# Second feed-forward product and second norm of a decoder layer: partial sums in a tile of their own, operand splits placed by another rule, norm bias copied in DRAM and added to by transfers, part of the statistics on ScalarE

## The chip, the cores and the metric

The kernel runs on one core of one Trainium2 chip. The metric is the device time of one execution in microseconds (us); the median of the runs shown is compared. The work is in float32: each matrix operand is held as a high and a low part (`both`, `wh`/`wl`, in fp32r), and each product is three matmuls (`mm3`, lines 113 to 115: high by high, high by low, low by high).

## The reference, cut to what matters

The layer normalises twice. The change is in the last two lines, `h @ w_ff2` and the second `layer_norm`.

```python
D_MODEL = 2048; SEQ = 512; D_FF = 4 * D_MODEL; ALPHA = 2 ** 0.25; LN_EPS = 1e-5

def layer_norm(x, gain, bias):
    mu = jnp.mean(x, axis=-1, keepdims=True)
    var = jnp.mean(jnp.square(x - mu), axis=-1, keepdims=True)
    return (x - mu) * lax.rsqrt(var + LN_EPS) * gain + bias

proj = x @ w_in[l]
...                      # gated recurrence, windowed attention, merged by gates
x = layer_norm(ALPHA * x + mixed @ w_out[l], ln1_gain[l], ln1_bias[l])
h = jnp.square(jax.nn.relu(x @ w_ff1[l])) @ w_ff2[l]
x = layer_norm(ALPHA * x + h, ln2_gain[l], ln2_bias[l])
```

## The kernel before

The stages run one after the other: projection of x, recurrence and attention, gates, `w_out` with the first norm, first feed-forward product, second feed-forward product, second norm. The instruction streams of the engines are laid out by a scheduler from the source; each engine then works through its stream in order, and SyncE (SP), ScalarE (ACT) and GpSimd (POOL) also issue transfers in their order.

**Start.** SyncE loads the first weight (`raw`, four pieces of 128 KB, line 97) and the first quarter of x (`xr`, four pieces of 256 KB, line 98), then x by 512 KB (line 185) and the weights by 512 KB (line 91). ScalarE writes the high part of each (`wh`, `both`, line 83), VectorE the low part (`wl`, line 84).

**Second feed-forward product** (from about 1950 us). The 512 tokens by 8192 rows of `h` lie in DRAM as `hd0` to `hd31`. There are 16 superblocks `s` of two `hd` each. For the output columns 0 to 1023 a superblock takes seven products instead of eight (`seven(s, i)`, i = 0 to 6; `product` makes 12 matmuls, of 128x512) on sums and differences of the operands. The columns 1024 to 2047 are done in the plain way, by `plain_unit` of 12 matmuls, one beside each `seven`. The operands of a superblock are made by `form(s, step)`: step -1 loads two `hd` into `raws[s]`, which is a pair tile for the first superblock and `HR0`, `HR1` (part of `slot`) for all others; steps 0 and 1 split them, 2 and 3 make sums, 4 and 5 split these. `A_RING` (four entries) and `S_RING` (two) hold the splits.

The results of the seven products are evacuated (`both_banks`: ACTIVATE at line 1052 or an addition at line 605) into four tiles `E`, `U2`, `T2`, `RX` of 128x1024, and `add_z` (line 956) adds them to `zq`, which holds the residual in DRAM, by accumulating transfers on GpSimd's queue. `E` serves two of them in each superblock: at i = 1 for `zq[0][0]` and at i = 4, as the partial sum U3, for `zq[1][1]`. ScalarE evacuates the plain columns' banks at line 1026.

**LAST** is the last plain block, columns 1536 to 2047 by the last three superblocks: 4 token tiles of 36 matmuls, straight in front of the second norm, with six weight tiles (`kept`).

**Second norm.** For each token tile `t` and column quarter `q`, `zq` is loaded to `zt[t, q]` on ScalarE's queue (line 1133). VectorE makes `bn_stats` of three quarters (line 1147), adds the bank `O[t]` of LAST to the fourth and makes its statistic (line 1149). `ln_core` gives the mean and 1/deviation (lines 830 to 838). Then mean, gain and bias are applied by all three of ScalarE (1156, 1160), VectorE (1157, 1159, 1164) and GpSimd (1159, 1161), and the quarters go out (line 1165). Gain and bias rows are loaded, broadcast, to E, U2, T2, RX (line 1136).

In the first feed-forward product the class `Sevens` uses tiles from `tmp` for partial sums, of 128x256.

## Time and profile before

| | us |
|---|---|
| median of 3 runs | 2648.18 |
| their range | 2646.94 to 2650.42 |
| the profiled execution | 2650.56 |
| its span in the trace | 2648.70 |
| TensorE busy in it | 2594.6 (98%) |
| VectorE, ScalarE, GpSimd busy | 1872.9, 1285.5, 261.4 |
| first matmul, last matmul's start | 5.00, 2625.86 |

The span is from the first to the last instruction of the profiled execution; its own time is 1.86 us longer. A row of a timeline gives the start, the duration, the engine, the source line, the operation with the tiles that it writes and reads, and in brackets how long the engine was idle before it and who released it. Queue rows (SPq, ACTq, POOLq) are transfers being issued. The busy time is an average over stages with different limits, so the places where TensorE is idle are looked up one by one.

### The profile page before, as it was taken

To read this page: it belongs to the slowest core of one execution; us is meant where nothing else is said; L and a number is where in the kernel's file an instruction comes from. 1 tells how busy PE (TensorE), PEld (TensorE's weight loads), DVE (VectorE), ACT (ScalarE), POOL (GpSimd) and SP (SyncE) were. 2 spreads that over 40 slices of the span, in tenths; PEclk is the share of its full clock that TensorE was granted. 3 is DMA by queue.
4 is the path that set the end of the run, shared out by engine and by line. 5 is a ranking of instruction groups with operands and counts; after the bars stand their busy time and mean duration, and the time that the engine had idled before them with its cause. 6 is when DMAs were issued, how large, how long until landed. Compare 5 with 4: busy or idle time off the path is not lost.

```text
span 2648.7 us, 36998 instructions
## 1 busy us (share of the span) xinstructions
PE 2594.6 (98%) x14624; PEld 2260.5 (85%) x14624; DVE 1872.9 (71%) x2531; ACT 1285.5 (49%) x1815; POOL 261.4 (10%) x276
## 2 busy tenths in 40 slices
PE   9999999999999999999999999999999999999995
PEld 8889888988888999988988999999988888877884
DVE  4588795574635888833768888888886777766756
ACT  4576655352433444422545455455565555544542
POOL 0110222130000000000300000000001111101112
PEclk9999999999999999999999999999999999999998
DMA  5222212222454555643552333333368887878866
GB/s 190 88 80 72 78 57 88 73 80 81 158 183 151 158 161 155 243 137 98 174 189 104 135 135 129 136 136 127 136 209 214 215 205 206 223 183 206 208 160 173
DMA packets 110318, 392.84 MB, mean 148 GB/s; under 512 B 12480, under 2 KB 13248, under 8 KB 109376
## 3 DMA queue, kind: packets, MB, share of 16 engines
q1 hardware_dynamic: 79200, 281.40, 31.6%
q0 software_dynamic: 24896, 91.24, 15.2%
q10 hardware_dynamic: 6048, 17.83, 2.1%
q8 instruction: 115, 1.88, 0.3%
q14 instruction: 59, 0.48, 0.1%
HBM read 299.19 MB, written 91.23 MB: 147 GB/s over the span
## 4 chain that ended last, share of the span: by engine, by line
PE 86%; DVE 5%; issue 4%; DMA 3%; ACT 1%; POOL 1%; SPq 0%; DVEq 0%; ACTq 0%; POOLq 0%
PE mm L115 17%; PE mm L113 16%; PE mm L114 16%; PE mm L662 8%; PE tp L662 5%; PE mm L664 4%; PE tp L114 4%; PE tp L113 4%; PE tp L115 4%; PE tp L664 2%; DMA zq<-slot 1%; PE sc L114 1%; PE sc L115 1%; PE sc L113 1%; DMA slot<-hd 1%
## 5 line engine op out<-in xcount | busy, mean ns | idle before, releaser
L83 ACT ACTIVATE wh<-raws 128x1024 fp32r<-128x1024 f32 x292 | 307.9, 1059 | 331.6 <-PE mm L114 107.5
L84 DVE TENSOR_TENSOR wl<-raw,wh 128x1024 fp32r<-128x1024 f32 (+1 forms) x183 | 221.4, 1210 | 306.0 <-PE mm L115 167.1
L84 DVE TENSOR_TENSOR wl<-raws,wh 128x1024 fp32r<-128x1024 f32 x292 | 354.3, 1220 | 61.4 <-ACT wh L83 51.7
L83 ACT ACTIVATE wh<-raw 128x1024 fp32r<-128x1024 f32 (+1 forms) x183 | 190.9, 1044 | 294.1 <-PE mm L114 142.7
L115 PE MATMUL mm<-both,wl 128*128 128x512 f32 (+1 forms) x912 | 331.0, 364 | 2.1 <-DVE wl L84 2.1
L113 PE MATMUL mm<-both,wh 128*128 128x512 f32 (+1 forms) x912 | 331.0, 364 | 2.0 <-ACT wh L83 1.2
L114 PE MATMUL mm<-both,wh 128*128 128x512 f32 (+1 forms) x912 | 331.3, 364 | 0.0
L662 PE MATMUL mm<-both,wh 128*128 128x512 f32 x896 | 321.8, 398 | 0.4 <-ACT wh L83 0.4
L664 PE MATMUL mm<-both,wl 128*128 128x256 f32 x896 | 251.3, 281 | 0.0
L113 PE MATMUL mm<-wh,both 128*128 128x256 f32 (+1 forms) x688 | 231.9, 340 | 5.7 <-ACT both L83 5.0
L114 PE MATMUL mm<-wl,both 128*128 128x256 f32 (+1 forms) x688 | 232.3, 338 | 4.2 <-DVE wl L84 4.2
L115 PE MATMUL mm<-wh,both 128*128 128x256 f32 (+1 forms) x688 | 231.0, 338 | 0.0
L662 PEld LDWEIGHTS mm<-both,wh 128*128 128x128 f32 x896 | 168.6, 188 | 37.6 <-ACT wh L83 0.6
L115 PEld LDWEIGHTS mm<-both,wl 128*128 128x128 f32 x912 | 172.0, 189 | 28.2 <-DVE wl L84 2.8
L113 PEld LDWEIGHTS mm<-both,wh 128*128 128x128 f32 x912 | 172.1, 189 | 28.0 <-ACT wh L83 1.4
L114 PEld LDWEIGHTS mm<-both,wh 128*128 128x128 f32 x912 | 172.2, 189 | 25.4 <-DVE both L84 0.2
L113 PE MATMUL mm<-xq,wh 128*128 128x256 f32 x672 | 190.4, 283 | 1.4 <-ACT wh L83 0.9
L115 PE MATMUL mm<-xq,wl 128*128 128x256 f32 x672 | 190.2, 283 | 0.1
L114 PE MATMUL mm<-xq,wh 128*128 128x256 f32 x672 | 190.1, 283 | 0.0
L664 PEld LDWEIGHTS mm<-both,wl 128*128 128x128 f32 x896 | 169.4, 189 | 0.5
L113 PEld LDWEIGHTS mm<-wh,both 128*128 128x128 f32 x688 | 131.4, 192 | 19.9 <-ACT both L83 5.0
L114 PEld LDWEIGHTS mm<-wl,both 128*128 128x128 f32 x688 | 131.6, 192 | 17.9 <-DVE wl L84 4.7
(313 smaller groups left out, 6082.0 us busy)
## 6 DMA issues: line engine op xcount, KB each, us to landing
raws<-w SPq DMA_DIRECT2D x178, 512.0 KB, 4.5
raw<-win SPq DMA_DIRECT2D x87, 512.0 KB, 3.6
zq<-slot POOLq DMA_DIRECT2D x63, 512.0 KB, 7.8
slot<-w SPq DMA_DIRECT2D x62, 512.0 KB, 6.1
raws<-wg SPq DMA_DIRECT2D x56, 512.0 KB, 4.4
raw<-wo SPq DMA_DIRECT2D x32, 512.0 KB, 3.6
hd<-r POOLq DMA_DIRECT2D x32, 512.0 KB, 2.9
zq<-r POOLq DMA_DIRECT2D x31, 512.0 KB, 8.3
```

Of the source, the lines that this page charges most:

```text
L83: ACT.activation(hi, src, AF.Copy)
L84: DVE.tensor_tensor(lo, src, hi.bitcast(F32), op=ALU.subtract)
L113: PE.matmul(o, ah, bh_, start=first, stop=False, skip_group_check=True)
L114: PE.matmul(o, ah, bl_, start=False, stop=False, skip_group_check=True)
L115: PE.matmul(o, al, bh_, start=False, stop=last, skip_group_check=True)
L662: PE.matmul(o[:].rearrange("p (i t) -> p i t", i=2), wh[:, k, :], x.two(k), start=first and k == 0, stop=False, skip_group_check=True)
L664: PE.matmul(o[:, :CG], wl[:, k, :], x.hi[:, k, :], start=False, stop=last and k == 7, skip_group_check=True)
```

## The change

1. `Sevens` takes its partial sums from one tile `sums` of five parts, instead of from five buffers of a pool.
2. In the second feed-forward product the partial sum U3 goes to the first four parts of `sums`, no longer to `E`.
3. `form` is called by another rule: the second superblock's operands go to a pair of their own, and from the fourth superblock on the steps are written one unit later. In the last superblock the products 5 and 6 change places.
4. Ahead of the product three DRAM tiles `od` are filled with the bias row of the second norm, one row for each of the 128 tokens. Of the first three token tiles, (x - mean) * gain / deviation is added to `od` by accumulating transfers, and `od` is then copied to the output. The fourth tile gets gain and bias on VectorE.
5. The statistics of two quarters of four per tile are made on ScalarE: a sum (ACTIVATE Copy), its negative, and a sum of squares around it (`triple`).
6. The loads of `zq` go to SyncE's queue.

```diff
-    def tmp(tag, bufs):
-        return pf.tile([P, CG], F32, tag=tag, bufs=bufs, name=nm(tag))[:]
+    sums = pf.tile([P, 5, CG], F32, name="sums")
+
+    def tmp(i, n):
+        return sums[:, i + n, :]
...
+    U3 = sums[:, :4, :].rearrange("p n t -> p (n t)")
...
         if step == -1:
-            if s < 1:
+            if s < 2:
...
-            both_banks(E, EA, False)
-            both_banks(E, EB, True)
-            add_z(1, 1, E)
+            both_banks(U3, EA, False)
+            both_banks(U3, EB, True)
+            add_z(1, 1, U3)
...
+    od = [pd.tile([P, D], F32, name=f"od{t}") for t in range(NT - 1)]
+    for o_ in od:
+        nc.scalar.dma_start(out=o_[:], in_=lnv[3, :].partition_broadcast(P))
+    st2 = pl.tile([P, NT, 6, 3], F32, name="st2")
+    for q in range(2):
+        DVE.memset(st2[:, :, q, 0:1], float(T))
...
-        v = u + 2
-        if v // 7 + 1 < NS and v % 7 < 6:
-            form(v // 7 + 1, v % 7)
-        if v % 7 == 6 and v // 7 + 2 < NS:
-            form(v // 7 + 2, -1)
-        seven(s, i)
+
+        if u < 4:
+            form(1, u + 2)
+        if 2 <= u < 8:
+            form(2, u - 2)
+        if s > 1 and i and s + 1 < NS:
+            form(s + 1, i - 1)
+        if i == 6 and 2 < s + 2 < NS:
+            form(s + 2, -1)
+        seven(s, i if s < NS - 1 else (0, 1, 2, 3, 4, 6, 5)[i])
...
-            nc.scalar.dma_start(out=zt[t, q], in_=zq[q][t // 2][:, t % 2, :])
-    for r in range(2):
-        for i in range(2):
-            nc.gpsimd.dma_start(out=gb2[2 * r + i], in_=lnv[2 + r, i * 1024:(i + 1) * 1024].partition_broadcast(P))
...
+            nc.sync.dma_start(out=zt[t, q], in_=zq[q][t // 2][:, t % 2, :])
+    for i in range(2):
+        nc.gpsimd.dma_start(out=(E, U2)[i], in_=lnv[2, i * 1024:(i + 1) * 1024].partition_broadcast(P))
+        nc.gpsimd.dma_start(out=(T2, RX)[i], in_=lnv[3, i * 1024:(i + 1) * 1024].partition_broadcast(P))
...
+    def triple(t, q):
+
+        junk, nmean = S_RING[(NS - 1) % 2][2][:, :T], pl.tile([P, 1], F32, tag="nmean", bufs=2, name=nm("nmean"))
+        ACT.activation(junk, zt[t, q], AF.Copy, scale=1.0 / T, accum_out=st2[:, t, q, 1:2])
+        ACT.activation(nmean[:], st2[:, t, q, 1:2], AF.Copy, scale=-1.0)
+        ACT.activation(junk, zt[t, q], AF.Square, bias=nmean[:], accum_out=st2[:, t, q, 2:3])
...
-        for q in range(3):
-            DVE.bn_stats(stats[:, t, q, :], zt[t, q])
-        tt(zt[t, 3], O[t][:], zt[t, 3], ALU.add)
-        DVE.bn_stats(stats[:, t, 3, :], zt[t, 3])
...
+        for q in range(2):
+            triple(t, q)
+        for q in range(2, 4):
+            if q == 3:
+                tt(zt[t, q], O[t][:], zt[t, q], ALU.add)
+            DVE.bn_stats(st2[:, t, 2 * q - 2:2 * q, :].rearrange("p a b -> p (a b)"), zt[t, q])
...
+        for q in range(4):
+            zc = zt[t, q]
+            DVE.scalar_tensor_tensor(zc, zc, mu, block_of((E, U2)[q // 2], q), op0=ALU.subtract, op1=ALU.mult)
+            if t < NT - 1:
+                ACT.activation(zc, zc, AF.Copy, scale=y)
+                nc.gpsimd.dma_start(out=od[t][:, q * T:(q + 1) * T], in_=zc, accum_op=ALU.add)
+            else:
+                DVE.scalar_tensor_tensor(zc, zc, y, block_of((T2, RX)[q // 2], q), op0=ALU.mult, op1=ALU.add)
+                (nc.sync if q % 2 else nc.scalar).dma_start(out=out[t * P:(t + 1) * P, q * T:(q + 1) * T], in_=zc)
+        if t < NT - 1:
+            nc.sync.dma_start(out=out[t * P:(t + 1) * P, :], in_=od[t][:])
```

What it moves is seen in the built order of each engine. A row has its place, the source line, the operation and its tiles.

**The start, ScalarE and SyncE.** ScalarE's first rows, before:

```order
1 L192 ACT_TABLE_LOAD
2 L192 ACTIVATE warm<-warm 128x1
3 L83 ACTIVATE wh_97<-raw_96 128x256
4 L83 ACTIVATE both<-xr_95 128x512
5 L83 ACTIVATE wh_97<-raw_96 128x256
```

and now (`lnv` holds the norms' rows, `od` the copies):

```order
1 L1095 DMA od_17607<-lnv 128x2048
2 L192 ACT_TABLE_LOAD
3 L192 ACTIVATE warm<-warm 128x1
4 L1095 DMA od_17608<-lnv 128x2048
5 L83 ACTIVATE wh_97<-raw_96 128x256
6 L1095 DMA od_17609<-lnv 128x2048
7 L83 ACTIVATE both<-xr_95 128x512
8 L83 ACTIVATE wh_97<-raw_96 128x256
```

The three copies stand between ScalarE's first instructions. SyncE's first loads with the semaphores that they wait for (DMAHW0 to 7 tell that a transfer has landed, and go round), before:

```order
5 L97 DMA raw_96<-win 128x256
6 L98 DMA xr_95<-xt 128x512
7 L97 DMA raw_96<-win 128x256
8 L98 DMA xr_95<-xt 128x512
9 L185 DMA xr_171<-xt 128x1024 [waits DMAHW0_49]
10 L185 DMA xr_171<-xt 128x1024 [waits DMAHW1_49]
11 L91 DMA raw_182<-win 128x1024 [waits DMAHW2_49]
```

and now:

```order
5 L97 DMA raw_96<-win 128x256
6 L98 DMA xr_95<-xt 128x512 [waits DMAHW0_49]
7 L97 DMA raw_96<-win 128x256 [waits DMAHW1_49]
8 L98 DMA xr_95<-xt 128x512 [waits DMAHW2_49]
9 L185 DMA xr_171<-xt 128x1024 [waits DMAHW3_49]
10 L185 DMA xr_171<-xt 128x1024 [waits DMAHW4_49]
11 L91 DMA raw_182<-win 128x1024 [waits DMAHW5_49]
```

The loads are the same, but three of the eight semaphores of the first round belong to the copies (0, 3 and 5), so that waiting begins three rows earlier.

**The middle, ScalarE**, where row 1447 is the evacuation at 2420.14 us of the trace before (`slot_17720` holds E, U2, T2 and RX, `slot_17721` the raw operands and weights):

```order
1446 L83 ACTIVATE wh_20939<-raws_20619 128x1024
1447 L1052 ACTIVATE slot_17720<-tp_17722 128x512
1448 L83 ACTIVATE both<-slot_17721 128x1024
1449 L1052 ACTIVATE slot_17720<-tp_17723 128x512
1450 L83 ACTIVATE wh_20958<-slot_17721 128x1024
1451 L1026 ACTIVATE slot_17720<-mm_17726 128x512
1452 L1026 ACTIVATE slot_17720<-mm_17727 128x512
1453 L83 ACTIVATE both<-slot_17721 128x1024
1454 L1052 ACTIVATE r_17731<-tp_17722 128x512
1455 L1052 ACTIVATE r_17731<-tp_17723 128x512
```

and now:

```order
1447 L83 ACTIVATE wh_20820<-raws_20498 128x1024
1448 L1055 ACTIVATE sums<-tp_17597 128x512
1449 L83 ACTIVATE both<-slot_17596 128x1024
1450 L1055 ACTIVATE sums<-tp_17598 128x512
1451 L83 ACTIVATE wh_20839<-slot_17596 128x1024
1452 L1029 ACTIVATE slot_17595<-mm_17601 128x512
1453 L1029 ACTIVATE slot_17595<-mm_17602 128x512
1454 L83 ACTIVATE both<-slot_17596 128x1024
1455 L1055 ACTIVATE r_17606<-tp_17597 128x512
1456 L1055 ACTIVATE r_17606<-tp_17598 128x512
```

The rows stand in the same order; two evacuations go to `sums` instead of `slot`.

**The end, VectorE**, the splits of LAST's weights (`wl`) and the first statistics, before:

```order
2322 L84 TENSOR_TENSOR wl_21978<-slot_17721,wh_21977 128x1024
2323 L1147 BN_STATS stats<-raws_22006 128x6
2324 L84 TENSOR_TENSOR wl_21983<-slot_17721,wh_21982 128x1024
2325 L605 TENSOR_TENSOR slot_17720<-tp_17724,slot_17720 128x512
2326 L605 TENSOR_TENSOR slot_17720<-sc_17725,slot_17720 128x512
2327 L84 TENSOR_TENSOR wl_21988<-slot_17721,wh_21987 128x1024
2328 L1147 BN_STATS stats<-raws_21996 128x6
2329 L84 TENSOR_TENSOR wl_21993<-slot_17721,wh_21992 128x1024
2330 L1147 BN_STATS stats<-raws_22001 128x6
2331 L1147 BN_STATS stats<-raws_22006 128x6
2332 L1147 BN_STATS stats<-raws_22011 128x6 x2
```

and now:

```order
2323 L605 TENSOR_TENSOR sums<-tp_17599,sums 128x512
2324 L605 TENSOR_TENSOR sums<-sc_17600,sums 128x512
2325 L84 TENSOR_TENSOR wl_21863<-slot_17596,wh_21862 128x1024
2326 L84 TENSOR_TENSOR wl_21868<-slot_17596,wh_21867 128x1024
2327 L605 TENSOR_TENSOR slot_17595<-tp_17599,slot_17595 128x512
2328 L605 TENSOR_TENSOR slot_17595<-sc_17600,slot_17595 128x512
2329 L84 TENSOR_TENSOR wl_21873<-slot_17596,wh_21872 128x1024
2330 L1177 BN_STATS st_17613<-raws_21881 128x6
2331 L84 TENSOR_TENSOR wl_21878<-slot_17596,wh_21877 128x1024
2332 L1177 BN_STATS st_17613<-raws_21886 128x6
2333 L1177 BN_STATS st_17613<-raws_21891 128x6
2334 L605 TENSOR_TENSOR raws_21881<-mm_17601,raws_21881 128x512
```

Of these rows two statistics stood ahead of a split (2323, 2328); now one does (2330), on the first token tile's third quarter, loaded from `zq`.

## Rows read from the trace of the kernel before

**Rows 1.** The page's first part, TensorE: busy us (share of the span) xinstructions

```profile
PE 2594.6 (98%) x14624; PEld 2260.5 (85%) x14624; DVE 1872.9 (71%) x2531; ACT 1285.5 (49%) x1815; POOL 261.4 (10%) x276
```

**Rows 2.** Timeline at the start: start us, us, engine, line, operation [idle before <-releaser]

```profile
5.00 0.58 PE L113 MATMUL mm<-wh,both 128*128 128x256 f32 x1 [5.00 <-ACT both L83]
...
13.18 1.06 ACT L83 ACTIVATE wh<-raw 128x1024 fp32r<-128x1024 f32 x1
```

**Rows 3.** Windows at the start: us, busy of each engine, PEclk, DMA share, GB/s

```profile
14.00:16.00 2.00, 0.95 (x5) 0.75 (x6) 1.73 (x2) 1.66 (x4) 0.00 (x0) 1.00 1.03 420
...
24.00:26.00 2.00, 2.00 (x19) 2.00 (x18) 0.01 (x1) 0.00 (x0) 0.00 (x0) 1.00 0.99 383
```

**Rows 4.** Timelines of TensorE, then ScalarE, in the second feed-forward product

```profile
2354.78 0.73 PE L113 MATMUL tp<-wh,both 128*128 128x512 f32 x2 [1.88 <-ACT wh L83]
...
2446.95 0.73 PE L113 MATMUL tp<-wh,both 128*128 128x512 f32 x2 [2.53 <-ACT wh L83]
...
2420.14 0.60 ACT L1052 ACTIVATE slot<-tp 128x512 f32<-128x512 f32 x1 [2.49 <-DMA zq<-slot]
...
2443.92 1.06 ACT L83 ACTIVATE both<-slot 128x1024 fp32r<-128x1024 f32 x1 [9.82 <-DMA slot<-hd]
```

**Rows 5.** Windows in the same product and at its end

```profile
2100.00:2110.00 10.00, 9.03 (x38) 6.63 (x37) 8.16 (x10) 3.41 (x5) 0.86 (x1) 1.00 0.68 188
2350.00:2360.00 10.00, 8.12 (x29) 6.20 (x28) 6.47 (x7) 5.68 (x7) 1.12 (x2) 0.83 0.51 108
...
2590.00:2600.00 10.00, 6.56 (x22) 4.87 (x21) 4.15 (x5) 3.77 (x5) 3.14 (x4) 0.83 1.03 222
```

**Rows 6.** Timeline of TensorE in LAST, from its first matmul to its last

```profile
2586.74 0.39 PE L113 MATMUL mm<-both 128*128 128x512 f32 x1
...
2594.79 0.80 PE L114 MATMUL mm<-wl,both 128*128 128x512 f32 x1 [3.44 <-DVE wl L84]
...
2601.92 0.50 PE L114 MATMUL mm<-wl,slot 128*128 128x512 f32 x1 [0.95 <-DVE wl L84]
...
2623.36 0.39 PE L113 MATMUL mm<-wh,slot 128*128 128x512 f32 x1
...
2625.86 0.39 PE L115 MATMUL mm<-wh,slot 128*128 128x512 f32 x1
```

**Rows 7.** Timelines of VectorE, then ScalarE, beside LAST

```profile
2592.92 0.69 DVE L1147 BATCH_NORM_STATS2 stats<-raws 128x6 f32<-128x512 f32 x1 [10.64 <-DMA raws<-zq]
2593.53 1.21 DVE L84 TENSOR_TENSOR wl<-slot,wh 128x1024 fp32r<-128x1024 f32 x1
...
2590.69 1.09 ACT L1026 ACTIVATE r<-mm 128x512 f32<-128x512 f32 x2
```

**Rows 8.** Timelines of VectorE, then ScalarE, behind the last matmul

```profile
2636.68 0.69 DVE L1149 BATCH_NORM_STATS2 stats<-raws 128x6 f32<-128x512 f32 x1
2637.41 0.26 DVE L830 BATCH_NORM_AGGREGATE mv<-stats 128x2 f32<-128x24 f32 x1
2637.71 0.15 DVE L831 TENSOR_SCALAR mv<-mv 128x1 f32<-128x1 f32 x1
...
2643.25 1.40 DVE L1164 SCALAR_TENSOR_TENSOR raws<-raws,mv,slot 128x512 f32<-128x512 f32 x2
...
2640.42 0.72 ACT L1160 ACTIVATE raws<-raws,mv 128x512 f32<-128x512 f32 x1 [0.42 <-DVE mv L837]
```

**Rows 9.** DMA issues: out<-in, queue, operation xcount, KB each, median us to landing

```profile
zq<-slot POOLq DMA_DIRECT2D x63, 512.0 KB, 7.8
...
z<-xn ACTq DMA_DIRECT2D x4, 1024.0 KB, 8.2
zq<-z POOLq DMA_DIRECT2D x16, 256.0 KB, 4.6
raws<-zq ACTq DMA_DIRECT2D x16, 256.0 KB, 7.7
...
out<-raws SPq DMA_DIRECT2D x8, 256.0 KB, 2.4
```

More of the change, by code (lines that the diff above doesn't have):

```diff
@@ L703, in group @@
             R = result()
-            E, U2, U3 = tmp("E", 2), tmp("U2", 2), tmp("U3", 1)
+            E, U2, U3 = tmp(0, self.n % 2), tmp(2, self.n % 2), tmp(4, 0)
             w = pair()
@@ L848, in ln1 @@
     def ln1(t):
-        _, y, b = ln_core(t)
+        _, y, b = ln_core(t, stats[:, t, :, :])
         for c in range(4):
@@ L1098, in layer @@
             form(1, -1)
+            form(2, -1)
         plain_unit(n)
@@ L1132, in layer, with block_of @@
             zt[t, q] = z[:, q // 2, (q % 2) * T:(q % 2 + 1) * T]
-            nc.scalar.dma_start(out=zt[t, q], in_=zq[q][t // 2][:, t % 2, :])
-    for r in range(2):
-        for i in range(2):
-            nc.gpsimd.dma_start(out=gb2[2 * r + i], in_=lnv[2 + r, i * 1024:(i + 1) * 1024].partition_broadcast(P))
-    g2 = [[gb2[2 * r + q // 2][:, (q % 2) * T:(q % 2 + 1) * T] for q in range(4)] for r in range(2)]
+            nc.sync.dma_start(out=zt[t, q], in_=zq[q][t // 2][:, t % 2, :])
+    for i in range(2):
+        nc.gpsimd.dma_start(out=(E, U2)[i], in_=lnv[2, i * 1024:(i + 1) * 1024].partition_broadcast(P))
+        nc.gpsimd.dma_start(out=(T2, RX)[i], in_=lnv[3, i * 1024:(i + 1) * 1024].partition_broadcast(P))
+    def block_of(v, q):
+        return v[:, (q % 2) * T:(q % 2 + 1) * T]
+    def triple(t, q):
[3 more added lines that the diff above has]
+        ACT.activation(junk, zt[t, q], AF.Square, bias=nmean[:], accum_out=st2[:, t, q, 2:3])
     for t in range(NT):
@@ L1145, in layer @@
                     n == 0 and k == 0, n == 2 * len(ss) - 1 and k == 1)
-        for q in range(3):
-            DVE.bn_stats(stats[:, t, q, :], zt[t, q])
-        tt(zt[t, 3], O[t][:], zt[t, 3], ALU.add)
-        DVE.bn_stats(stats[:, t, 3, :], zt[t, 3])
-        mu, y, _ = ln_core(t)
-        zcs = [zt[t, c] for c in range(4)]
-        gs, bs_ = g2
-        nmu = pl.tile([P, 1], F32, tag="nmu", bufs=2, name=nm("nmu"))
-        DVE.tensor_scalar(nmu[:], mu, -1.0, None, op0=ALU.mult)
-        for c in (3, 1, 2):
-            ACT.activation(zcs[c], zcs[c], AF.Identity, bias=nmu[:])
-        DVE.scalar_tensor_tensor(zcs[0], zcs[0], mu, gs[0], op0=ALU.subtract, op1=ALU.mult)
-        for c in (3, 1, 2):
-            (POOL if c == 3 else DVE).tensor_tensor(zcs[c], zcs[c], gs[c], op=ALU.mult)
-        ACT.activation(zcs[3], zcs[3], AF.Copy, scale=y)
-        POOL.tensor_tensor(zcs[3], zcs[3], bs_[3], op=ALU.add)
-        for c in range(4):
-            if c < 3:
-                DVE.scalar_tensor_tensor(zcs[c], zcs[c], y, bs_[c], op0=ALU.mult, op1=ALU.add)
-            (nc.sync if c % 2 else nc.scalar).dma_start(out=out[t * P:(t + 1) * P, c * T:(c + 1) * T], in_=zcs[c])
+        for q in range(2):
[4 more added lines that the diff above has]
+            DVE.bn_stats(st2[:, t, 2 * q - 2:2 * q, :].rearrange("p a b -> p (a b)"), zt[t, q])
+        mu, y, _ = ln_core(t, st2[:, t, :, :].rearrange("p a b -> p (a b)"))
+        for q in range(4):
[9 more added lines that the diff above has]
+            nc.sync.dma_start(out=out[t * P:(t + 1) * P, :], in_=od[t][:])
 def _constants():
```

5 lines of the change are left out of this document (2 added, 3 removed).

## The prediction

> **What bounds the kernel now.** I read the page's busy shares first, then the windows at start and end, then the waits inside them. TensorE is busy 98% of the span [rows 1], and its 14,624 matmuls stay as they are, so the change can only move the few places where TensorE stands still. There are three.
>
> The start. The first matmul starts at 5.00 us, and the weight of the second chunk is split at 13.18 [rows 2], as it lands. The DMA engines' share of their time is 1.03 at 14 to 16 us and still 0.99 at 24 to 26 [rows 3]. So the first 26 us have no spare transfer time, and TensorE is fed by transfers there.
>
> The middle. Three stalls in the second feed-forward product: about 1.0 us (9.03 busy of 10 at 2100 to 2110 [rows 5]), 1.88 and 2.53 us [rows 4]. The last comes through ScalarE: its queue stands 9.82 us for an `hd` load, ahead of the evacuations and the split that TensorE wants [rows 4]. Where TensorE stood 1.88 us, its granted clock is 0.83 over ten microseconds [rows 5], some 3 us at half speed of them, which costs about 1.5 us more.
>
> The end. The last plain block, LAST (144 matmuls, four token tiles of 36), starts at 2586.74. At the pitch of 0.227 us (2623.36 to 2625.86 is eleven) it needs 32.6 us and would end at 2619.4; it ends at 2626.3. The 6.9 us between are a wait of 3.44, one of 0.95 and slow matmuls behind the first [rows 6]. Both waits are for VectorE's `wl`; ahead of the first, VectorE stands 10.64 us for a load of `zq`, with a statistic [rows 7]. From the last matmul it is 22.4 us to the span's end, bound by VectorE, which then has more than two tiles to normalise.
>
> **The change, part by part**, against the profiled run (2650.56 us: span 2648.70 and 1.86 around it), then carried over to the median of 2648.18.
>
> *Bias rows copied in DRAM, at the start.* Three copies to `od`, each 128 rows of 8 KB, 1 MB. In the source they stand ahead of the second feed-forward product, but they wait for nothing, and the order puts them at the top of ScalarE's queue, between its first splits. 3.15 MB at the 420 GB/s of 14 to 16 us [rows 3] are 7.5 us of all engines, in a stretch without spare time: nothing hides them. They also hold SyncE's queue: completion semaphores go round in eight, so the third piece of x waits until the first copy has landed, the first 512 KB piece for the second copy, the second chunk's weight for the third. Upper bound: all of it goes ahead of the second chunk's weight, 7.5, and TensorE stands long enough to run slowly again, 1.5: 9. Lower bound: by then 3.15 MB of x and weights must land, with the copies 6.3 MB, 15.0 us from about 2 us on, so 17.0 instead of 13.18, where later loads shared the engines: 3.8. I take **+6**, nearer the upper end, since the copies' rows of 8 KB are longer than the pieces they run against. Later chunks shift along: TensorE is busy 2.00 of 2 us at 24 to 26 [rows 3]. The small constants that now go ahead of the fourth weight, and two memsets, fall into that stretch: nothing.
>
> The Trainium skill, DMA: Bandwidth & Descriptors, section Rules for kernel authors, says to issue a DMA early and to wait for it late. By that the start would cost nothing (rival 2); the engines' share of 1.03 speaks against it here [rows 3].
>
> *Later operands.* In the source the splits of a superblock's operands move by a step. In the built order they don't: from the fourth superblock on, ScalarE's splits from `slot` and SyncE's `hd` loads stand where they stood, since they are placed when ring and buffers come free. Only the first three superblocks differ (the second gets a pair of its own). I give it 0, between -1 and +1; the stalls of 1.0 and 1.88 us stay.
>
> *An own place for the partial sum.* An evacuation waited for the accumulating transfer that still read the shared tile, as at 2420.14 for 2.49 us [rows 4]. Now it writes `sums`, and what is queued behind it on ScalarE comes forward by as much, up to the `hd` load whose split at 2443.92 holds TensorE, if that load's buffer comes free along this chain. Lower end 0 (another engine frees it), upper end 2.53 + 1.5 = 4. I take **-2**.
>
> *LAST.* The loads of `zq` go from ScalarE's to SyncE's queue, so that splits no longer stand behind them; the last two products change places; two statistics of four per tile become pairs of ACTIVATEs. But VectorE's order still has one statistic on a loaded `zq` ahead of the split of the sixth weight tile, which LAST needs at its 31st matmul, 6.8 us in. The `zq` add for it is ready 30 matmuls, 6.8 us, before LAST, less 1.1 for the evacuation [rows 7]: 5.7. It lands 7.8 us later, is loaded in 2.4 to 7.7 [rows 9], then 0.69 + 1.21 on VectorE [rows 7]: ready 6.4 to 11.7 us into LAST. The stall is 0 to 5, and 1.5 of slow clock where it is over 1.9. I take 3.5 for both, in place of 6.9: **-3.4**.
>
> *The tail.* POOL's eight tensor operations and VectorE's products with them go. For the last tile, behind the last matmul: sum and statistic 0.69 each, aggregation 0.26, six small ones of 0.15, eight scalar-tensor operations of 0.70, then what stood behind the last one before, from 2644.65 to 2648.70, 4.05: 12.2 us [rows 8]. The third tile takes a longer way: VectorE 5.3 us, so done 2.9 us ahead of the last matmul (its own last one lies 36 matmuls, 8.2 us, ahead); four ACTIVATEs of 0.72 [rows 8], 2.9; accumulating transfers of 256 KB, 4.6 us; then SyncE copies 1 MB from DRAM to DRAM, 8.2 us by the nearest row, 4.3 if it has the engines alone (2.4 for the first 256 KB [rows 9], the rest at 420 GB/s); and 1.6 to the end (4.05 less an output's 2.4): 14.4, or 10.5. I take **13.0** for the later of the two ways, nearer to the upper row since the last tile's outputs run beside it, in place of 22.4: **-9.4**.
>
> Sum: 6 - 2 - 3.4 - 9.4 = -8.8. Profiled run 2641.8, median **2639.4 us**.
>
> **The rivals.**
> 1. *The copies cost more, and the kernel gets slower.* No row of before shows a copy from DRAM to DRAM. The stretch that accumulating transfers fill (2590 to 2600) moves 222 GB/s at a share of 1.03 [rows 5]; at that rate 3.15 MB take 14.2 us. All of it ahead of the second chunk's weight, 1.5 for TensorE slow again, 2.2 more for the copy of 1 MB at the end: 17.9 - 14.8 = +3.1, 2651.3. It decides from a price of 14.8 on; 5.3 above that it would be measured as slower, at some 165 GB/s. For it: SyncE's queue is held meanwhile. Against it: rows of 8 KB, and no addition.
> 2. *The copies hide* behind TensorE's first chunk: the start costs 0 to 1, and -14.8 to -13.8 give 2634. Against it: the shares of 0.99 to 1.03 [rows 3].
> 3. *The end is not won.* The statistic ahead of the sixth split holds LAST as long as before, 6.9; the third tile's way takes 14.4; the middle gives 0: 6 - 8.0 = -2.0, 2646.2. For it: POOL now waits for the landing of the add that reads RX before it loads a bias block there, and the last two adds of `zq` stand behind that.
> 4. *It doesn't do what it says in the middle*: the operands move nothing, as the order shows, and if the own place does nothing either, 2641.4. This lies inside the forecast.
>
> The Trainium skill, DMA: Bandwidth & Descriptors, section Specifications, puts a core's share of DRAM traffic at about 358 GB/s. With read and written bytes both under it the three copies would take 17.6 us, and the sum would be +2.8, close to rival 1. The 420 GB/s of [rows 3] are above that figure, but for reads alone.
>
> **How the numbers follow.** Forecast with rival 4: 0.43 (own range 2636 to 2643). Rival 1: 0.23, rival 2: 0.13, rival 3: 0.21. Within 0.2%, about what a measurement of this kernel tells from no change, is 2642.9 to 2653.5. Faster: 0.38 of the forecast and rival 2: 0.51. Slower: the upper half of rival 1, 0.13, and a little of rival 3: 0.15. Same: 0.34. The range of 2633 to 2651 leaves out the upper half of rival 1 and the far end of rival 2.
>
> **What would show it.** Right: the first matmul at 7 to 9 us and the second chunk's weight split at 17 to 21; a DMA share of 1 up to about 33 us; no wait of ScalarE for `zq` in the middle, with the stalls of 1.0 and 1.88 us in place; LAST 33 to 38 us long; the last matmul 11 to 15 us before the end, and the third tile's copy among the last two to land. Wrong: copies that land after 20 us, a wait inside LAST above 5 us, a tail above 16, or new stalls in the first three superblocks, where the order did change.

## The result, and the profile after

| | before | after |
|---|---|---|
| median, us | 2647.56 (6 runs, 2644.33 to 2651.20) | 2660.59 (6 runs, 2657.57 to 2667.24) |
| ratio to before | | 1.0054 (95% interval 1.0042 to 1.0067) |
| profiled execution, us | 2650.56 | 2660.39 |
| its span, us | 2648.7 | 2658.6 |

The changed kernel is slower by some 13 us, where 8.8 us less were predicted, and the time lies above the range. The profiled execution is close to the median, so its rows can be taken for the loss. Both kernels issue 14,624 matmuls; how much later the matmul of the same number starts in one trace than in the other tells how much was lost up to there:

| stretch | predicted, us | shift in the two profiled executions, us |
|---|---|---|
| start (to the 400th matmul) | +6 | +8.7 |
| from there to the second feed-forward product | 0 | +0.3 |
| second feed-forward product | -2 | -2.5 |
| LAST | -3.4 | -4.5 |
| start of the last matmul to the span's end (22.8 before, 30.7 after) | -9.4 | +7.9 |
| sum | -8.8 | +9.9 |

**The start.** The timeline of after, ScalarE's queue and ScalarE, then TensorE (start us, us, engine, line, operation, idle before and releaser):

```profile
0.73 0.61 ACTq L1095 DMA_DIRECT2D od<-lnv  x1
...
9.78 0.63 ACT L83 ACTIVATE both<-xr 128x512 fp32r<-128x512 f32 x1 [6.33 <-DMA xr<-xt]
...
21.74 1.06 ACT L83 ACTIVATE wh<-raw 128x1024 fp32r<-128x1024 f32 x1
```

```profile
10.46 0.58 PE L113 MATMUL mm<-wh,both 128*128 128x256 f32 x1 [10.46 <-ACT both L83]
...
16.49 0.39 PE L113 MATMUL mm<-wh,both 128*128 128x256 f32 x1 [3.10 <-ACT both L83]
...
22.85 0.50 PE L113 MATMUL mm<-wh,both 128*128 128x256 f32 x2
24.11 0.39 PE L114 MATMUL mm<-wl,both 128*128 128x256 f32 x1 [0.76 <-DVE wl L84]
```

In before, the first matmuls of the second chunk:

```profile
14.29 0.50 PE L113 MATMUL mm<-wh,both 128*128 128x256 f32 x2 [0.71 <-ACT wh L83]
15.55 0.39 PE L114 MATMUL mm<-wl,both 128*128 128x256 f32 x1 [0.76 <-DVE wl L84]
```

And the windows of after there (us, busy time of each engine, TensorE's granted clock, DMA share, GB/s):

```profile
4.00:6.00 2.00, 0.00 (x0) 0.00 (x0) 0.00 (x0) 0.00 (x0) 0.00 (x0) 1.00 0.94 285
...
18.00:20.00 2.00, 2.00 (x11) 2.00 (x10) 1.40 (x4) 1.35 (x3) 0.00 (x0) 0.50 1.01 408
...
30.00:32.00 2.00, 2.00 (x19) 2.00 (x18) 1.24 (x6) 0.22 (x1) 0.00 (x0) 1.00 0.98 370
32.00:34.00 2.00, 2.00 (x19) 2.00 (x18) 0.00 (x0) 0.66 (x1) 0.00 (x0) 1.00 0.64 256
```

The first matmul starts at 10.46 in place of 5.00, the second chunk's weight is split at 21.74 in place of 13.18 [rows 2]. The DMA engines are full until 32 us (shares of 0.93 to 1.08); only the window behind that shows 0.64. TensorE stands 3.10 us for a piece of x, and its granted clock at 18 to 20 us is 0.50, the lower of its two levels (1.2 GHz). The matmul behind the second chunk's `wl` starts at 24.11; in before it starts at 15.55. That is 8.56 us.

**The middle and LAST.** TensorE's waits of after that answer to [rows 4, 6], and VectorE beside the last of them:

```profile
2366.37 0.73 PE L113 MATMUL tp<-wh,both 128*128 128x512 f32 x2 [2.25 <-ACT wh L83]
...
2455.05 0.73 PE L113 MATMUL tp<-wh,both 128*128 128x512 f32 x2 [0.66 <-ACT wh L83]
...
2602.36 0.50 PE L114 MATMUL mm<-wl,slot 128*128 128x512 f32 x1 [1.95 <-DVE wl L84]
```

```profile
2600.48 0.69 DVE L1177 BATCH_NORM_STATS2 st<-raws 128x6 f32<-128x512 f32 x1 [6.67 <-DMA raws<-zq]
2601.09 1.21 DVE L84 TENSOR_TENSOR wl<-slot,wh 128x1024 fp32r<-128x1024 f32 x1
```

The stall of 1.88 us is still there (2.25), the one of 2.53 has shrunk to 0.66, and LAST has one wait of 1.95 where it had 3.44 and 0.95. It is the predicted one: VectorE's statistic on a loaded `zq` stands ahead of the split that TensorE needs. What the two executions also differ in is TensorE's clock around such waits, first before (the wait of 2.53), then after (those of 2.25 and 1.95):

```profile
2446.00:2456.00 10.00, 9.05 (x33) 7.29 (x34) 9.96 (x13) 5.88 (x7) 0.86 (x1) 0.83 0.45 77
```

```profile
2362.00:2372.00 10.00, 7.75 (x35) 6.09 (x34) 6.88 (x7) 6.53 (x8) 1.52 (x2) 1.00 0.45 93
2600.00:2605.00 5.00, 3.06 (x14) 2.19 (x13) 2.42 (x3) 0.00 (x0) 0.00 (x0) 1.00 1.05 227
```

In before the granted clock is 0.83 in the ten microseconds around three waits, those of 1.88 and 3.44 [rows 5] and that of 2.53. By estimate that is 1.7 us each time (0.17 of 10). In after it is 1.00 in both places, and over the whole second product.

**The tail.** Timelines of after around and behind the last matmul (2627.88 to 2628.3): VectorE and ScalarE, GpSimd's queue, then SyncE's queue.

```profile
2633.90 2.73 DVE L1186 SCALAR_TENSOR_TENSOR raws<-raws,mv,slot 128x512 f32<-128x512 f32 x4
...
2628.53 2.56 ACT L1183 ACTIVATE raws<-raws,mv 128x512 f32<-128x512 f32 x4 [0.81 <-DVE mv L839]
```

```profile
2618.25 3.50 POOL L1184 DMA_DIRECT2D od<-raws  x4 [11.00 <-ACT raws L1183]
2626.08 7.10 POOL L1184 DMA_DIRECT2D od<-raws  x8 [4.33 <-ACT raws L1183]
```

```profile
2628.68 21.56 SPq L1189 DMA_DIRECT2D out<-od  x3
2650.35 0.98 SPq L1187 DMA_DIRECT2D out<-raws  x2
```

DMA issues of after (out<-in, queue, count, KB each, median us to landing), what SyncE's queue waited for (us in total, times, longest), and the windows:

```profile
od<-raws POOLq DMA_DIRECT2D x12, 256.0 KB, 9.6
out<-raws ACTq DMA_DIRECT2D x2, 256.0 KB, 8.8
...
out<-od SPq DMA_DIRECT2D x3, 8.2
```

```profile
SPq L1189 <- DMA od<-raws: 36.5, 3, 16.8
```

```profile
2615.00:2620.00 5.00, 5.00 (x24) 4.14 (x23) 4.44 (x12) 4.90 (x12) 1.75 (x3) 1.00 0.14 11
2620.00:2625.00 5.00, 5.00 (x24) 4.14 (x23) 4.26 (x13) 4.78 (x16) 1.75 (x2) 1.00 1.01 122
2625.00:2630.00 5.00, 3.26 (x15) 2.37 (x13) 4.07 (x11) 4.19 (x10) 3.92 (x5) 1.00 1.01 138
...
2640.00:2645.00 5.00, 0.00 (x0) 0.00 (x0) 0.00 (x0) 0.00 (x0) 0.00 (x0) 0.50 1.61 404
2645.00:2650.00 5.00, 0.00 (x0) 0.00 (x0) 0.00 (x0) 0.00 (x0) 0.00 (x0) 0.50 0.21 36
```

VectorE is done at 2636.6, 8.3 us behind the end of the last matmul (2628.3). Then nothing computes for 22 us. From 2620 to 2630 the accumulating transfers fill all 16 engines (share 1.01), and these move 122 to 138 GB/s, a third of the 408 at the same share at the start. Their median time to landing is 9.6 us; the first takes 4.9, the last 18.2. SyncE's queue waits 36.5 us in three pieces for them before its copies, so that the third copy leaves at 2650.2; the last tile's two outputs stand behind it on the same queue and leave from 2650.35 on, though VectorE had them 14 us before. In the last five microseconds of that wait the engines are nearly idle (0.21, 36 GB/s): a full queue explains the wait up to about 2645 and not its end, which no run takes apart.

### The profile page after: what moved, and what is told of

It reads as the page before. It is cut to its first block, busy times and chain, and to the rows that moved or that the text cites. A ratio compares the mean times of both kernels' runs of the same rounds, so it can differ in the third digit from the quotient of the medians.

```text
span 2658.6 us, 37012 instructions
## 1 busy us (share of the span) xinstructions
PE 2591.9 (97%) x14624; PEld 2258.8 (85%) x14624; DVE 1858.0 (70%) x2517; ACT 1296.2 (49%) x1851; POOL 260.2 (10%) x280
## 3 DMA queue, kind: packets, MB, share of 16 engines
q8 instruction: 115, 1.88, 0.3%
## 4 chain that ended last, share of the span: by engine, by line
PE 87%; DVE 4%; DMA 4%; ACT 2%; issue 2%; POOL 1%; DVEq 0%; ACTq 0%; POOLq 0%; SPq 0%
PE mm L115 17%; PE mm L113 17%; PE mm L114 17%; PE mm L664 8%; PE tp L664 5%; PE mm L666 4%; PE tp L113 4%; PE tp L114 4%; PE tp L115 4%; PE tp L666 2%; DMA slot<-hd 2%; DMA zq<-slot 1%; PE sc L114 1%; PE sc L115 1%; PE sc L113 1%
## 5 line engine op out<-in xcount | busy, mean ns | idle before, releaser
L114 PEld LDWEIGHTS mm<-wl,both 128*128 128x128 f32 x688 | 131.3, 191 | 14.2 <-DVE wl L84 1.0
```

The lines of the kernel that those rows point to most:

```text
L114: PE.matmul(o, ah, bl_, start=False, stop=False, skip_group_check=True)
```

## The experiments

The theory after the result: the loss comes from the bias rows by transfers and from nothing else, in two places, at the start (the copies into `od`) and at the end (accumulating transfers, copies out, what is queued behind them). The rivals: the new statistics on ScalarE, the moved loads or the order in the second product cost time; at the start the loss is in completion semaphores and not in bytes; at the end it is in the queue order and not in the accumulation. Each ratio below is against runs of the kernel before on the same chip (its 95% interval in brackets); the medians of before there are 2646.5 to 2648.2.

**Without the transfers.** Copies, accumulating transfers and copies out are gone, VectorE adds the bias for all four tiles:

```diff
-    for o_ in od:
-        nc.scalar.dma_start(out=o_[:], in_=lnv[3, :].partition_broadcast(P))
...
-            if t < NT - 1:
-                ACT.activation(zc, zc, AF.Copy, scale=y)
-                nc.gpsimd.dma_start(out=od[t][:, q * T:(q + 1) * T], in_=zc, accum_op=ALU.add)
-            else:
+            if True:
                 DVE.scalar_tensor_tensor(zc, zc, y, block_of((T2, RX)[q // 2], q), op0=ALU.mult, op1=ALU.add)
...
-        if t < NT - 1:
-            nc.sync.dma_start(out=out[t * P:(t + 1) * P, :], in_=od[t][:])
```

> The changed kernel without the od copies: no copies at the start, no accumulating transfers into od, no copies from od to the output; VectorE multiplies and adds gain and bias for all four tiles, as it does for the fourth. Theory A (the bias by accumulating transfers costs at both ends: +8.9 us at the start, and a tail that is bound by twelve transfers of 256 KB, one behind the other from 2618 to 2650): first matmul back at 5.0, second chunk's low part back at 15.6, the last matmul about 22 us before the end as in the kernel before (VectorE 8 us a tile) or better, since the statistics start earlier; 2637 to 2645 us, 16 to 23 below the changed kernel. Theory B (the tail is long because VectorE and ScalarE are behind, not the transfers): the tail gets longer than 31 us, since VectorE has 2.7 us more for each of three tiles; 2652 to 2660.

Measured: 2641.04, 0.9979 (0.9968 to 0.9990), inside the first range. The whole loss is in the transfers, and the rest of the change gains some 5.5 us. The `wl` matmul at the start is back at 15.64, the tail is 19.3 us. VectorE now bounds it; its timeline in this kernel:

```profile
2618.86 0.24 DVE L832 BATCH_NORM_AGGREGATE mv<-st 128x2 f32<-128x18 f32 x1
...
2626.80 0.24 DVE L832 BATCH_NORM_AGGREGATE mv<-st 128x2 f32<-128x18 f32 x1
...
2630.63 2.73 DVE L1180 SCALAR_TENSOR_TENSOR raws<-raws,mv,slot 128x512 f32<-128x512 f32 x4
```

A tile takes 7.94 us (2618.86 to 2626.80), about as long as its 36 matmuls, 8.2.

**The copies into `od` later.** GpSimd issues them at three places of the first feed-forward product, each behind a small transfer that waits for that place; the end is left as in the change:

```diff
     for g in range(NHEAD, NG):
         sevens.group(g, w1[g])
+        t, r = divmod(g - NHEAD - 4, 5)
+        if r == 0 and 0 <= t < NT - 1:
+            nc.gpsimd.dma_start(out=od[t][:, 0:8], in_=sums[:, 2 + sevens.n % 2, 0:8])
+            nc.gpsimd.dma_start(out=od[t][:], in_=lnv[3, :].partition_broadcast(P))
```

> The changed kernel with the three od copies made in the middle of the first feed-forward product, on GpSimd's queue, where the transfer engines are busy a third of their time; nothing else differs but the first rows of ScalarE and SyncE. Theory A: the start is as in the kernel before (second chunk's low part at 15.6), the tail stays at 30.7 us from the last matmul's start; 2651.7 us (2650 to 2654), 8.9 below the changed kernel. Theory B says the same of the start. Rival for the start (the shift comes from the order of the first rows, not from the copies' bytes): less than 4 us of gain.

Measured: 2652.00, 1.0019 (1.0006 to 1.0031), as expected. So the place of the copies is worth 8.6 us (2660.59 - 2652.00, give or take some 4 by the intervals), as the shift at the start says, and the transfers at the end 11.0 (2652.00 - 2641.04, same chip). Mid-kernel a copy costs TensorE nothing: in the windows around the three it is busy 10.00 of 10 us. The window around the first, and their line among the DMA issues:

```profile
1466.00:1476.00 10.00, 10.00 (x64) 8.94 (x63) 6.43 (x9) 4.52 (x6) 0.99 (x3) 1.00 0.59 214
```

```profile
od<-lnv POOLq DMA_DIRECT2D x3, 1024.0 KB, 6.8
```

**Bytes or semaphores at the start.** The same copies at the start, from GpSimd's queue, so that SyncE's loads of x share no completion semaphore with them:

```diff
     for o_ in od:
-        nc.scalar.dma_start(out=o_[:], in_=lnv[3, :].partition_broadcast(P))
+        nc.gpsimd.dma_start(out=o_[:], in_=lnv[3, :].partition_broadcast(P))
```

> The changed kernel with the three od copies issued from GpSimd's queue at the same time at the start, so that they share no completion semaphore with SyncE's loads, which are then all issued as in the kernel before. If the start's 8.9 us are the copies' bytes: the shift stays at 7 to 9 us, 2659 to 2661 us. If they are SyncE's queue held by the semaphores: the shift falls to 4 us or less, 2653 to 2656.

Measured: 2658.91, 1.0049 (1.0034 to 1.0063), at the lower end of the first range: bytes. TensorE's timeline of this kernel:

```profile
5.62 0.58 PE L113 MATMUL mm<-wh,both 128*128 128x256 f32 x1 [5.62 <-ACT both L83]
...
13.75 0.58 PE L113 MATMUL mm<-wh,both 128*128 128x256 f32 x1 [5.21 <-ACT both L83]
...
23.98 0.39 PE L114 MATMUL mm<-wl,both 128*128 128x256 f32 x1 [0.71 <-DVE wl L84]
```

The first matmul is nearly where it was in before (5.00), yet the second chunk's `wl` comes at 23.98, as in after (24.11). The held queue only decides which piece is late first.

**Plain writes in place of the accumulating ones.** Same bytes, same queue. This kernel leaves out the bias of three token tiles, so it is an experiment and no version:

```diff
-                nc.gpsimd.dma_start(out=od[t][:, q * T:(q + 1) * T], in_=zc, accum_op=ALU.add)
+                nc.gpsimd.dma_start(out=od[t][:, q * T:(q + 1) * T], in_=zc)
```

> The changed kernel with its twelve transfers into od as plain writes instead of accumulating ones: the bias is left out for three token tiles. Bytes, queues, waits and order are the same. Theory A, in its sharper form (it is the adding in DRAM that is slow, 0.25 to 0.3 us for a row of 2 KB on each engine, so that twelve transfers fill all engines for some 29 us): plain rows of 2 KB took 0.085 us, the twelve keep up with ScalarE, and the tail falls from 30.7 us to 15 to 18, as the prediction had it; 2644 to 2648 us. Rival D (the chain of write, copy and output, each with its landing time, is what is long): the tail falls by less than 5 us, 2656 to 2660.

Measured: 2650.23, 1.0008 (0.9998 to 1.0018), between the two ranges and nearer the first: some 10 us of the change's loss (2660.59 - 2650.23) go with the addition alone, and the start is unchanged (+8.8). The tail is 17.9 us where it was 30.7. Its windows and its transfers:

```profile
2615.00:2620.00 5.00, 5.00 (x24) 4.14 (x23) 4.72 (x11) 4.94 (x14) 2.19 (x4) 1.00 0.53 184
2620.00:2625.00 5.00, 5.00 (x24) 4.14 (x23) 4.66 (x11) 4.84 (x13) 1.02 (x2) 1.00 0.68 237
```

```profile
od<-raws POOLq DMA_DIRECT2D x12, 256.0 KB, 5.0
```

Here 237 GB/s take a share of 0.68, by estimate some 350 at a full share; with the addition a full share moved 122 to 138.

**One accumulating transfer per tile**, with rows of 8 KB in place of four with rows of 2 KB:

```diff
-                nc.gpsimd.dma_start(out=od[t][:, q * T:(q + 1) * T], in_=zc, accum_op=ALU.add)
+                if q == 3:
+                    nc.gpsimd.dma_start(out=od[t][:], in_=zw[t][:].rearrange("p a b -> p (a b)"), accum_op=ALU.add)
```

> The changed kernel with one accumulating transfer for each of three tiles, of rows of 8 KB, in place of four of rows of 2 KB; the copies at the start stay. If an accumulating transfer costs by its rows (2 KB rows took about 0.3 us each on each engine), the three take far less: the tail shrinks from 30.7 to 18 to 22 us, 2648 to 2652 us. If it costs by its bytes (about 110 GB/s), the tail stays and the later start of the first piece makes it slightly longer: 2659 to 2663. Theory B (VectorE and ScalarE are behind): no change, 2660.

Measured: 2658.41, 1.0041 (1.0025 to 1.0056), just below the second range, 2 us better than the change by the medians, which the intervals don't tell from nothing. Its add for the first tile, the copy that waits for it, and the three adds' median:

```profile
2623.03 0.85 POOL L1186 DMA_DIRECT2D od<-raws  x1 [13.15 <-ACT raws L1184]
...
2630.94 19.86 SPq L1191 DMA_DIRECT2D out<-od  x3
```

```profile
od<-raws POOLq DMA_DIRECT2D x3, 1024.0 KB, 11.1
```

The first tile's add is cheaper: 7.9 us from its issue to the copy (2623.03 to 2630.94), where the four of the change took 10.4 (2618.25 to 2628.68). The windows of that tail from 2625 to 2645 show shares of 0.74 to 1.02 in place of 1.01. But the chain stays: the third add leaves at 2634.33, 2.5 us behind the last matmul's start, lands 16.0 us later (the median of the three is 11.1), its copy out follows, and the last tile's outputs leave SyncE's queue at 2650.89. The tail is 27.3 us.

**The last tile's outputs past that queue**, all four on ScalarE's:

```diff
-                (nc.sync if q % 2 else nc.scalar).dma_start(out=out[t * P:(t + 1) * P, q * T:(q + 1) * T], in_=zc)
+                nc.scalar.dma_start(out=out[t * P:(t + 1) * P, q * T:(q + 1) * T], in_=zc)
```

> The changed kernel with all four outputs of the last tile on ScalarE's queue, so that none stands on SyncE's queue behind the copies from od, which wait for the accumulating transfers. Theory A: the two outputs that landed last (issued at 2650.4, landed at 2657.5) go, the copy of the third tile is then the last: 3 us less, 2657 to 2659. Rival C (SyncE's queue order is what makes the tail long): 8 us less or more, 2650 to 2653.

Measured: 2656.47, 1.0035 (1.0022 to 1.0049): some 4 us less than the change by the medians, just below the first range and well above the rival's. The queue order is a part, and not the main one: the third tile's own copy still leaves late (SyncE's queue is 22.22 us at its copies), and the outputs, though issued at 2632, take 12.2 us in place of 2.4 [rows 9], among the accumulating transfers.

**The parts that should gain.** Three kernels try one part each. The own place of the partial sum and the operands' order, taken back on top of the kernel without transfers (the diff shows the first; the old calls of `form` come back too, the swapped last products stay):

```diff
-    U3 = sums[:, :4, :].rearrange("p n t -> p (n t)")
+    U3 = E
...
```

> As the run without od copies, with the middle as before: the partial sum back in the shared tile, and the operands by the old rule. If the own place is worth the 2.5 us between the two profiled middles: 2643.5 us, 2.5 above the run without od. Rival: the stalls in the middle come and go from one execution to the next (the profiled middles so far hold 0.6 to 6 us of stalls with the same order), and the middle is worth nothing: 2640 to 2642.

Measured: 2641.26, 0.9967 (0.9955 to 0.9979), not slower than with them (0.9979), so the rival's range holds: worth nothing that can be measured. Then the statistics, all four of a tile on VectorE again, on top of the same kernel:

```diff
-        for q in range(2):
-            triple(t, q)
-        for q in range(2, 4):
+        for q in range(4):
...
```

> As the run without od copies, with all four statistics of a tile on VectorE. There VectorE bounds the tail with 7.9 us a tile, and the two statistics that come back cost 1.4 us a tile where nothing hides them: the first tile's and some of the next ones are made while VectorE waits for loads, the last ones' are not. Theory A: 2643 to 2646 us, 2 to 5 above. Rival (they are all made early, while VectorE waits): 2641.

Measured: 2641.32, 0.9971 (0.9959 to 0.9982): also nothing, and again the rival's time. And the kernel before with only the loads of `zq` moved to SyncE's queue:

```diff
-            nc.scalar.dma_start(out=zt[t, q], in_=zq[q][t // 2][:, t % 2, :])
+            nc.sync.dma_start(out=zt[t, q], in_=zq[q][t // 2][:, t % 2, :])
```

> The kernel before with its sixteen loads of zq on SyncE's queue, and nothing else. If the gain in LAST (4.5 us between the two profiled runs) comes from ScalarE's splits that no longer stand behind loads: 2643 us, 4 to 5 below the kernel before. If it comes from the swapped products or from fewer statistics on VectorE ahead of the splits: 2646 to 2648, as before.

Measured: 2645.97, 1.0001 (0.9992 to 1.0010): nothing, the rival's side once more.

**The one part that does.** The kernel before, with mean, gain and bias of each tile by VectorE alone; GpSimd's eight operations and ScalarE's with them are gone:

```diff
-        for c in (3, 1, 2):
-            (POOL if c == 3 else DVE).tensor_tensor(zcs[c], zcs[c], gs[c], op=ALU.mult)
...
-        POOL.tensor_tensor(zcs[3], zcs[3], bs_[3], op=ALU.add)
...
+            DVE.scalar_tensor_tensor(zc, zc, mu, gs[c], op0=ALU.subtract, op1=ALU.mult)
+            DVE.scalar_tensor_tensor(zc, zc, y, bs_[c], op0=ALU.mult, op1=ALU.add)
```

> The kernel before with mean, gain and bias applied by VectorE alone, as in the run without od copies, in place of VectorE, ScalarE and GpSimd; loads, statistics, products and order of the middle as before. A tile then takes VectorE 8 operations of 0.66 us and the statistics, 7.9 to 8.0 us, against 8.6 with VectorE held up beside GpSimd. Theory E (the gain of the run without od copies lies in GpSimd's leaving, 0.7 us a tile, and in the rest of LAST and the tail): 2644 to 2646 us, 2 to 3 below the kernel before. Rival (all of the 6 us are this): 2641.

Measured: 2643.02, 0.9982 (0.9971 to 0.9992), 5.2 us below the kernel before on that chip, more than the 2 to 3 expected and near the rival's 6; it lies within the interval of the kernel without transfers. VectorE takes over the operations of the others and is sooner done: a tile takes 7.06 us where it took 8.61 in before (2628.80 to 2637.41 [rows 8]), and the tail is 17.5 us. The aggregations of this kernel, then the one of before:

```profile
2622.35 0.26 DVE L830 BATCH_NORM_AGGREGATE mv<-stats 128x2 f32<-128x24 f32 x1
...
2629.41 0.26 DVE L830 BATCH_NORM_AGGREGATE mv<-stats 128x2 f32<-128x24 f32 x1
```

```profile
2628.80 0.27 DVE L830 BATCH_NORM_AGGREGATE mv<-stats 128x2 f32<-128x24 f32 x1
```

A reason is in the rows of the kernel before, GpSimd's timeline beside VectorE's:

```profile
2630.24 1.27 POOL L1159 TENSOR_TENSOR raws<-raws,slot 128x512 f32<-128x512 f32 x1 [2.63 <-ACT raws L1156]
2632.61 1.56 POOL L1161 TENSOR_TENSOR raws<-raws,slot 128x512 f32<-128x512 f32 x1 [1.10 <-ACT raws L1160]
```

```profile
2630.27 1.25 DVE L836 SCALAR_TENSOR_TENSOR mv<-mv 128x1 f32<-128x1 f32 x1
...
2631.64 0.68 DVE L1159 TENSOR_TENSOR raws<-raws,slot 128x512 f32<-128x512 f32 x1
...
2632.97 1.75 DVE L1159 TENSOR_TENSOR raws<-raws,slot 128x512 f32<-128x512 f32 x1
```

The same product takes 0.68 us alone and 1.75 while GpSimd's operation runs (2632.61 to 2634.17), and an operation on a single column, 0.16 elsewhere, takes 1.25 and ends with GpSimd's (2630.24 to 2631.51). That is about 1.1 us twice in each of the last two tiles. The Trainium skill, SBUF — State Buffer, section SBUF: two separate sides, has GpSimd and VectorE share a pair of ports that the first to start holds for a whole instruction, also against a VectorE operation with two SBUF inputs while GpSimd's reads SBUF; these rows agree. The run takes GpSimd's and ScalarE's operations away together, so that GpSimd's are the cause is read from the rows and not isolated.

**Towards a better version.** Late copies and one wide add per tile, for two tiles only, with the outputs of the other two on ScalarE's queue:

```diff
-            if t < NT - 1:
+            if t < NT - 2:
                 ACT.activation(zc, zc, AF.Copy, scale=y)
```

> A version drawn from the runs: od for two tiles only, filled in the middle of the first feed-forward product, one accumulating transfer of 8 KB rows for each, the other two tiles by VectorE, all direct outputs on ScalarE's queue. Theory A: the two adds and their copies (about 5 us of all engines and 3 to 5 us of copying each, from 2608 on) are done before VectorE is, which saves 2.7 us for each of two tiles: 2634 to 2637 us, 4 to 7 below the run without od. If even two adds hold the end: 2640 or more.

And for the first tile alone, with its copy out on GpSimd's queue:

```diff
-            if t < NT - 1:
+            if t < 1:
                 ACT.activation(zc, zc, AF.Copy, scale=y)
...
-            nc.sync.dma_start(out=out[t * P:(t + 1) * P, :], in_=od[t][:])
+            nc.gpsimd.dma_start(out=out[t * P:(t + 1) * P, :], in_=od[t][:])
```

> As the run without od copies, but the first token tile's bias by one accumulating transfer of 8 KB rows into od, which is filled in the middle of the first feed-forward product; add and copy to the output on GpSimd's queue, so that neither SyncE's queue nor the shared semaphores hold an output. Add and copy are over by about 2630, before VectorE ends. Theory A: VectorE is spared 2.7 us, 2638 to 2639 us, 2 to 3 below the run without od. If one add and its copy already hold the other outputs: 2641 or more.

Measured: two tiles 2647.68, 0.9995 (0.9983 to 1.0007), a miss of more than 10 us, on the side that the expectation gave for two adds that hold the end; one tile 2640.04, 0.9974 (0.9964 to 0.9983), a little above what was expected. The second beats both kernels and can't be told from the one without transfers (0.9979). With two tiles VectorE is done at 2632.8, but ScalarE's queue stands on the last outputs:

```profile
2630.82 11.13 ACTq L1191 DMA_DIRECT2D out<-raws  x4
```

The built order says on what the last of the four waits, ahead of it the second copy out on SyncE's queue:

```
L1193 DMA out<-od_12414 16x16384 [waits DMAHW1_49,DMASW1_49]
L1191 DMA out<-raws_21896 128x512 [waits DMAHW1_49,DVE_49]
```

Both use the completion semaphore `DMAHW1`. The copy left at 2633.2 and took 8.3 us, so that the output could leave at 2641.6 only. No run took this wait alone away.

## Why the prediction was wrong, point by point

**The tail is the step that failed**: -9.4 was forecast and +7.9 measured, and the sign of being wrong that was named for it, a tail above 16 us, is there. The last tile's way was right (VectorE done 8.3 us behind the last matmul; predicted 12.2 less 4.05 for the output, 8.15), and so was the reading that the third tile's way is the longer one. It was put together as nothing left at the last matmul's end, 4.6 for the accumulating transfers, 8.2 for the copy and 1.6 to the end, of which 13.0 was taken. It became 2.8 (ScalarE's scaling of that tile ends at 2631.1), 19.1 (the copy leaves at 2650.2) and 8.4 to the span's end: 30.3. The mis-sized term is the 4.6, for two reasons. The first is that its row does not add: `zq<-z` [rows 9] is line 861 of the kernel before, a plain write,

```python
            nc.gpsimd.dma_start(out=zq[c][t // 2][:, t % 2, :], in_=zc)
```

with no `accum_op`. The plain writes of the experiment came near it, 5.0 us; the row of before that adds is `zq<-slot`. The second is that 4.6 is the way of a single transfer; twelve were queued within 15 us, and a queue is priced by what the engines move. The trace of before had a row for that: 222 GB/s at a full share where accumulating transfers run beside loads [rows 5]. The prediction used it for the copies, which add nothing, and not for the transfers that add. At that rate twelve times 256 KB (3.15 MB) take 14.2 us, and with that in place of 4.6 the sum of -8.8 would have been +0.8. At the 130 GB/s of after, the middle of 122 and 138, they take 24.2, and the sum +10.8, where the spans differ by +9.9. That this comes so near is luck in part, since the first of the twelve left 10 us ahead of the last matmul's end. With the additions turned into plain writes the tail was 17.9, so the term would have been -4.9: a smaller error remains in the way without them, where the last outputs take about 8.4 us among copies and writes in place of 2.4 [rows 9].

**The start** had the right mechanism and sign: all engines busy, and nothing hides the copies. +6 was taken and +8.6 measured (by the medians), close to the upper bound of 9. So nearly all three copies went ahead of the second chunk's weight. That bound was 7.5 for the bytes and 1.5 for TensorE slow again, and the lower clock did come; but it shows no cost of its own. In before TensorE waits 0.71 us for the second chunk's `wh` (14.29), in after there is no such wait (22.85), so the slow matmuls of the first chunk ended as the weight was split. The 8.56 us are then the transfers' alone: 3.15 MB at an estimated 370 GB/s in place of 420. The held SyncE queue, which the text gave beside the bytes, is not the price: without it the shift is the same. The first matmul was expected at 7 to 9 and came at 10.46, the split at 17 to 21 and came at 21.74. Issued in the middle of the kernel, where the engines' share with them was 0.59 to 0.74, the copies cost TensorE nothing, and that is still some 1000 us ahead of their use. The Trainium skill, DMA: Bandwidth & Descriptors, section Rules for kernel authors, advises to issue a DMA early and to wait for it late, so that its fixed setup cost overlaps. In this case the earliest place cost 8.6 us more than the later one.

**The middle**: ScalarE's wait for `zq` is gone, the stall behind it went from 2.53 to 0.66, and the shift of -2.5 fits the -2. But this is luck. The two stretches of lower clock in before, which after doesn't have, are by estimate 3.4 us of TensorE's time, more than the whole shift; and the prediction's 1.5 us of slow clock behind a stall over 1.9 did not come behind the 2.25 of after. Five kernels with the same order up to LAST (the change, wide adds, outputs on ScalarE, plain writes, copies by GpSimd) have shifts from -1.7 to -8.2 in this stretch, one profiled execution each; and two that keep the order of before there (loads of `zq` on SyncE, VectorE alone in the tail) have -4.0 and -3.4. So the profiled execution of before stood longer there than is usual, and some of what the prediction read was this execution's own. Undoing both parts costs nothing that the runs can tell (intervals of 0.0012 either way, some 3 us). The term should have been near 0, with several us of spread in any one profile.

**LAST**: the wait is where it was predicted, 1.95 in place of up to 5, and -4.5 was measured for -3.4. Of the -4.5, by estimate 1.7 are the lower clock, which after doesn't have behind its wait. The same five kernels show -0.5 to -4.5 here, the kernel with two tiles a wait of 3.69. Whether any of it is gained stays open: neither the moved loads nor the moved statistics gain anything measurable by themselves, and the run with VectorE alone in the tail, which has none of these parts, can't be told from the kernel without transfers (0.9982 and 0.9979).

**The rivals.** The first had the right sign and asked the right thing, what happens if the transfers cost more, but put its price on the copies, of which the forecast already had most. The third, an end that is not won, was nearest in place, and named GpSimd's loads and the sixth split, which are not it. The second, copies that hide, fell. The fourth, a middle that does nothing, holds as far as the runs can tell.

**What was gained** comes from a part that the prediction only named in passing ("POOL's eight tensor operations and VectorE's products with them go"): the tail by VectorE without the other two, worth 5.2 of the 5.5 us by the medians, within the noise all of them. That the stretched VectorE operations are the reason is read from the rows.

The balance by the medians: copies at the start +8.6, transfers at the end +11.0, the rest, above all the other engines out of the tail, -5.5 (0.0021 of 2646.5); together +14, with +13.0 measured. The sum is no check of the parts, since each is the difference between one kernel and the next; only the chips differ.

## What to carry to other kernels

Price a transfer that stands in a queue by the bytes that all engines move per microsecond in a row of the same kind, and keep accumulating transfers apart from plain ones, by the source line and not by the tiles' names; the landing time of a single one is only a lower bound. A transfer that depends on nothing was put at the front of this program, where the loads that feed the first matmuls have no time to spare: give it a dependency that puts it where the engines have room. And a stall, or a stretch of lower clock, read from one profiled execution is worth no more than its spread over executions, so an edit that aims at it is priced near 0 until several traces show it.

## What the runs showed of the hardware

Accumulating transfers of 256 KB with 2 KB rows into DRAM keep 16 DMA engines full at 122 to 138 GB/s (the change, 2620 to 2630); plain writes of the same shape move 237 at a share of 0.68. A first tile of 1 MB is added in 7.9 us with rows of 8 KB and in 10.4 with rows of 2 KB, one execution each. A 1 MB copy of rows within DRAM takes 10.2 us at the full start and 6.8 in the middle of the kernel (medians of three). An operation of VectorE on one column took 1.25 us in place of 0.16 while GpSimd worked on SBUF. Around waits of TensorE of 1.88, 2.53 and 3.44 us one execution shows a granted clock of 0.83 over ten microseconds; around waits of 2.25 and 1.95 another shows 1.00.
